# Four row tiles of activations in one tile, combined sets made 1280 columns at a time, and one accumulator copy moved to ScalarE

## The chip, the cores and the metric

The kernel runs on one core of one Trainium2 chip. The metric is the device time of one execution in microseconds; the figure for a kernel is the median of several runs. TensorE (PE) multiplies, VectorE (DVE) and ScalarE (ACT) do elementwise work, GpSimd (POOL) a little of it, and SyncE (SP) issues most DMAs. Each engine takes its instructions in the order in which they were written and waits on semaphores; here that order is written out by hand.

## The reference

One step of a hybrid diffusion backbone with one layer: 128 context tokens and 512 latent tokens, 640 in all, of 1024 channels, in float32.

```python
def trunk_layer(x, cond, ...):
    mod = jax.nn.silu(cond) @ w_mod + b_mod            # 9 vectors of 1024
    sh1, sc1, g1, shm, scm, gm, sh2, sc2, g2 = jnp.split(mod, N_MOD, axis=-1)
    h = modulate(rmsnorm(x, norm_g[0]), sh1, sc1)
    x = x + 0.5 * g1[:, None, :] * swiglu(h, ffn1_w1, ffn1_w2)     # 1024 -> 2 x 2816 -> 1024
    h = modulate(rmsnorm(x, norm_g[1]), shm, scm)
    y, C, n, m = mixer(h, ...)                         # w_in: 1024 -> 9232, mLSTM, conv, gates
    x = x + gm[:, None, :] * y
    h = modulate(rmsnorm(x, norm_g[2]), sh2, sc2)
    x = x + 0.5 * g2[:, None, :] * swiglu(h, ffn2_w1, ffn2_w2)
    return x, C, n, m
```

Context tokens use one conditioning vector and latent tokens another. A last RMSNorm ends it; the states of the mLSTM's context scan are outputs too.

## The kernel before

**Layout.** Activations lie transposed: 1024 channels are 8 row tiles (k = 0 to 7) of 128 partitions, 640 tokens are columns, cut into two halves (h = 0, 1) of 320 (`HT`). A matmul has 128 x 128 weights and 320 moving columns. Each float32 operand is split into a rounded high part and a remainder (`split`: a cast on ScalarE, L75, then a subtraction on VectorE, L79), and `three` makes one product out of three matmuls (L245 to L247).

**The pair element.** Most products with 1024 input channels come two column blocks at a time (`pair_el`, `pair_steps`), by a scheme of seven block products instead of eight. The activations are a 2 x 2 block matrix: blocks "11" and "21" (channels 0 to 511 and 512 to 1023 of half 0), "12" and "22" (the same of half 1). Besides these the scheme needs four combined sets, each of four row tiles: T1 = 12 - 11, T2 = 22 - T1, T3 = 22 - 12, T4 = 21 - T2. Weights are combined in the same way (L218) and split (L75, L79), four operands ahead of their use (`AHEAD`). A pair takes seven products of twelve matmuls, in the order A11, S1, S2, A12, S3, S4, A22, which use the activation sets 11, T1, T2, 21, T3, 22, T4. Between them accumulators are copied: after A11 its accumulator is copied to b (L273, ScalarE), on which S2 goes on; after S2, b is copied to c (L283, ScalarE), on which S3 and then A22 go on. After S3 the accumulator c is read, with S1's result added, into `c22`: by VectorE out of PSUM (L294), or with `spare_v` by a ScalarE copy (L291) and a VectorE addition (L292). A22 may write c only when that reading is done. `ev` then takes each result (L963 the silu on ScalarE, L965 the product on VectorE).

**The head of a stage.** Where a stage starts (first FFN, mixer, second FFN) the normalised activations are not ready yet, and the combined sets still have to be made. So the first blocks are made with plain products (`first_head` for the first FFN, `head_el` for the others): first half 0, then half 1, one unit of 24 matmuls for each block and half. While they run, `some`, called at two points of each unit, takes items off the list `work` that `right_chain` made: t1 (L905), the splits of T1, and so on, at a pace that spreads the list evenly over the points (12 in the first FFN, 10 in the others). In the first FFN the order is t1, T1, t3, T3, t2, T2, t4 and, after the head, T4. In the mixer and the second FFN it is t1, T1, t2, T2, t3, T3; t4 and T4 are in `N["later"]` and are issued (`fill`) between the products of the first pair. t2 is L908, t3 L911, t4 L914; t1, t2 and t4 are all made in place in one set `N["T"]`, t3 in place of half 1's channels 0 to 511. Items pushed on `lazy` (the splits of U, the gated products) go out at the next pair or step.

**Storage.** A row tile is one tile of 128 x 320, from rotating buffers: `utile` gives the normalised activations N[h, k] and N["T", k] (24 buffers, `Uh` and `Ul`, which the FFN's U tiles share), `hpair` the high and low tiles of a set (4 buffers each). The H tiles serve as scratch elsewhere: `YB` (mixer output), `h_wide` (accumulators), `FN` and `YT` (final norm).

Of the kernel before, what the change touches and what calls it, by code (L numbers as in the profile page):

```python
# [12 lines left out]
P = 128  # L13
# [31 lines left out]
def mixer_step(ctx: ExitStack, tc: tile.TileContext, x_prompt, x_sample, state_C, state_n, state_m,  # L45
# [28 lines left out]
    def split(raw, hi, lo, owe=False):  # L74
        A.copy(hi, raw)  # L75
        if owe:
            owed.append(lambda: V.tensor_sub(lo, raw, f32(hi)))
        else:
            V.tensor_sub(lo, raw, f32(hi))  # L79
# [693 lines left out]
    sq, SQ = {}, []  # L773
    PIECES = ((0, 128, 192), (320, 448, 512))
    OPS_H = ("11", "21", "22", "T1", "T2", "T3", "T4")
    cnt = {"u": 0}

    def utile():
        cnt["u"] += 1
        return PO["u"].tile([P, HT], F32, name=("Uh", "Ul")[cnt["u"] % 2], bufs=12)  # L780

    def hpool(o):
        return PO["hq"] if o in ("T1", "T2", "T3") else hp

    def hpair(o):
        return (hpool(o).tile([P, HT], F32R, name="H" + o + "h", bufs=4),
                hpool(o).tile([P, HT], F32R, name="H" + o + "l", bufs=4))

    def square(m, h):
        a, b = HALVES[h]  # L790
# [45 lines left out]
            PE.matmul(p[:, dst:dst + n], ones, dg[:, :n], start=True, stop=True)  # L836
        return p

    N = {}

    def scale_x(h, k, rb, engine=V):
        a, b = HALVES[h]
        t = utile()
        engine.tensor_mul(t, X[k][:, a:b], rb[:, :HT])  # L844
        N[h, k] = t

# [7 lines left out]
                V.tensor_scalar(t[:, a:b], t[:, a:b], sc_, bi_, op0=OP.mult, op1=OP.add)  # L854

    def put(o, kk, src):
        HB.setdefault(o, [None] * 4)[kk] = hl = hpair(o)
        split(src, *hl)

    def left_lists(n, sh):  # L860
        sc_ = lambda *ks: [lambda k=k: scale_x(0, k, N["rb", 0]) for k in ks]
# [16 lines left out]
    def right_chain(n, sh):  # L878

        def all_of(*fs):  # L880
            def f():
                for x in fs:
                    x()
            return f

        def right(k):
            if k < 4:
                HB.setdefault("12", [None] * 4)[k] = hl = hpair("T4")
                split(N[1, k], *hl)
            else:  # L890
                put("22", k - 4, N[1, k])

        def rows(k0, k1):

            for k in range(k0, k1):
                if k < KT:
                    scale_x(1, k, N["rb", 1])
                if 1 <= k <= KT:
                    modulate(1, k - 1, n, sh)
                if k >= 2:  # L900
                    right(k - 2)

        def t1(k):
            N["T", k] = utile()
            V.tensor_sub(N["T", k], N[1, k], N[0, k])  # L905

        def t2(k):
            V.tensor_sub(N["T", k], N[1, k + 4], N["T", k])  # L908

        def t3_(k):  # L910
            V.tensor_sub(N[1, k], N[1, k + 4], N[1, k])  # L911

        def t4(k):
            V.tensor_sub(N["T", k], N[0, k + 4], N["T", k])  # L914
        ks = range(4)
        work = [lambda k=k: t1(k) for k in ks] + [lambda k=k: put("T1", k, N["T", k]) for k in ks]
        work += [lambda k=k: t3_(k) for k in ks] + [lambda k=k: put("T3", k, N[1, k]) for k in ks]
        work += [lambda k=k: t2(k) for k in ks] + [lambda k=k: put("T2", k, N["T", k]) for k in ks]
        work += [lambda k=k: t4(k) for k in ks]
        last = [lambda k=k: put("T4", k, N["T", k]) for k in ks]  # L920
        if n in (1, 2):

            N["later"] = [all_of(*p) for p in zip(work[24:28:2], work[25:28:2])] + [all_of(*p) for p in zip(last[::2], last[1::2])]
            work, last = work[:8] + work[16:24] + work[8:16], []
        def fetch():

            if n == 2:
                A.activation(tp.tile([P, 3], F32, name="rstd", bufs=2)[:, 0:1], eps, AF.Silu)

        chain = [stat_fn(1), all_of(rows_fn(1), fetch, lambda: rows(0, 6)), lambda: rows(6, 9), lambda: rows(9, 10)]  # L930
        return chain + last, work
# [19 lines left out]
    def ffn(w1, w2, g, lists, head_of, n_head, e1=None):  # L951

        head, els, f0 = [], [], 0
        for size in GROUPS:
            U = {}
            grp = []
            for j in range(size):
                sa = {}

                def ev(mi, h, src, sa=sa, j=j, U=U):  # L960
                    if mi == 0:
                        sa[h] = t3()
                        A.activation(sa[h], src, AF.Silu)  # L963
                    else:
                        V.tensor_mul(sa[h], src, sa[h])  # L965

                        def put_u():
                            U[j, h] = hl = (PO["u"].tile([P, HT], F32R, name="Uh", bufs=12),
                                            PO["u"].tile([P, HT], F32R, name="Ul", bufs=12))
                            split(sa[h], *hl)  # L970
                        lazy.append(put_u)
                p = (w_load(w1, 0, KT, (f0 + j) * P, 2 * DFF), w_load(w1, 0, KT, DFF + (f0 + j) * P, 2 * DFF), ev)
                if f0 + j < n_head:
                    head.extend(blocks_of(p))
                else:
                    grp.append(pair_el(*p, e1 if f0 == 0 else None))
            acts = lambda k, h, U=U: U[k, h]
            ld = lambda m, f0=f0, size=size: w_load(w2, f0 * P, size, m * P, D)
            last = f0 + size == NFF
            w2s = [plain_el(ld(m), size, acts, lambda h, ps, m=m, last=last: add_x(m, h, ps, g, last))  # L980
                   for m in range(KT if not last else 2)]
            w2s[0] = dict(w2s[0], calm=False)
            if last:
                w2s.append(halves_el([ld(m) for m in range(2, KT)], size, acts,
                                     lambda m, h, ps: add_x(m + 2, h, ps, g, True), lists))
            els.append((grp, w2s))
            f0 += size
        return head_of(head), els
# [74 lines left out]
    def first_put(h, *ks):  # L1063
        for k in ks:
            if h == 0:
                put("11" if k < 4 else "21", k % 4, N[0, k])
            elif k < 4:
                HB.setdefault("12", [None] * 4)[k] = hl = hpair("T4")
                split(N[1, k], *hl)
            else:  # L1070
                put("22", k - 4, N[1, k])
# [786 lines left out]
    def sc_ev(m):  # L1858
        def ev(h, ps):
            g = GS[m][:, hsl(h)]  # L1860
            t = TL[m, h]
            V.tensor_mul(g, ps, g)
            V.scalar_tensor_tensor(t, t, 0.5, g, op0=OP.mult, op1=OP.add)
            if h == 0:
                return
            for i in range(2):
                YB[m, i] = hpair(YO[i][m // 4])
                split(TL[m, i], *YB[m, i])
            if m:
                x_in(m - 1)  # L1870
        return ev
# [5 lines left out]
    def m_wide():  # L1877
        return [xp.tile([P, T], F32, name="x", bufs=KT)[:, :512]]

    def h_wide():  # L1880
        return [hpool(o).tile([P, HT], F32, name="H" + o + "h", bufs=4)[:, :256] for o in ("T1", "T2")]

    def open_u2():
        m2.close()
# [36 lines left out]

    def fn_in():
        for q in range(4):
            t = hpool(OPS_H[q]).tile([P, HT], F32, name="H" + OPS_H[q] + "h", bufs=4)
            G.dma_start(t[:, :256], dap(final_norm, q * 256, [[0, P], [1, 256]]))
            FN.append(t)

    def y_part(m, h):
        def f():
            p = aux()  # L1930
            for i, a in enumerate(PIECES[h]):
                PE.transpose(p[:, i * P:(i + 1) * P], X[m][:, a:a + P], ident)
            q = m // 2
            for i in range(3):
                if h:
                    if m == 0:
                        YT[1, i] = ring.tile([P, 1024], F32, name="wr", bufs=RAWB)
                    V.tensor_mul(YT[1, i][:, m * P:(m + 1) * P], p[:, i * P:(i + 1) * P],
                                 FN[q][:, (m % 2) * P:(m % 2 + 1) * P])
                    continue  # L1940
                if m % 2 == 0:
                    YT[h, i, q] = hpool(OPS_H[q]).tile([P, HT], F32,
                                                       name="H" + OPS_H[q] + "h", bufs=4)
                V.tensor_mul(YT[h, i, q][:, (m % 2) * P:(m % 2 + 1) * P], p[:, i * P:(i + 1) * P],
                             FN[q][:, (m % 2) * P:(m % 2 + 1) * P])
        return f
# [41 lines left out]

    PO["y"] = y_queue
    head, els = ffn(ffn2_w1, ffn2_w2, G2, y_after, lambda bl: head_el(bl, *right_chain(2, SH2), mod_mid(G2, 0)), 2)  # L1990
    els[0][0][0]["fill"] = [step(f) for f in N["later"] + [lambda: None] * 6]
    prog += [head] + els[0][0] + [step(half_gate(G2))]
    for i in range(3):
        prog += els[i][1] + els[i + 1][0]
# [30 lines left out]
```

## Time and profile before

| | |
|---|---|
| median of 3 runs | 1662.68 us (1661.75 to 1663.08) |
| profiled execution | 1662.47 us, its span 1660.7 us |
| TensorE (PE) busy | 1641.4 us, 99%, 11189 matmuls |
| VectorE (DVE) busy | 1262.8 us, 76%, 2690 instructions |
| ScalarE (ACT) busy | 793.7 us, 48%, 1729 instructions |
| GpSimd (POOL) busy | 170.8 us, 10% |
| mean granted TensorE clock | 0.999 |

The span runs from the first to the last instruction. A row of the timeline begins with the start and the duration in us, then the engine, the line of the kernel, the operation, output tile <- input tiles, the shape and how many were merged into the row; in brackets stand the idle time of the engine before it and what ended that. In the groups by line the numbers behind the bar are busy us, mean ns of one, and idle time before. In a table of stages the columns are the span and the busy time of PE, its weight loads, DVE, ACT and POOL (with counts), the granted clock, the share of DMA and GB/s. Matmuls are pipelined and overlap, so their spacing is read from their starts.

### The profile page before, as it was taken

The page shows a single profiled execution, that of the slowest core. Times are in us where ns is not written, and L with a number is a line of the kernel's source. Part 1 is how long each engine was busy: PE and PEld are TensorE (multiplying, and loading weights), DVE is VectorE, ACT ScalarE, POOL GpSimd, SP SyncE. Part 2 cuts the span into 40 slices and gives each one's busy share as a digit, 9 for nine tenths or more (in the row PEclk, how much of TensorE's full clock was granted, in tenths as well). Part 3 has the DMA queues.
Part 4 walks back from the last instruction along what each step waited for, and adds up shares of the span by engine and source line. Part 5 has one row for each costly group of instructions (what it writes and reads, how often), then busy time and mean ns, then how long its engine had stood idle before and what let it go on. Part 6 is the DMA issues. An engine that isn't in the chain of part 4 may idle for free.

```text
span 1660.7 us, 29312 instructions
## 1 busy us (share of the span) xinstructions
PE 1641.4 (99%) x11189; PEld 1599.5 (96%) x11189; DVE 1262.8 (76%) x2690; ACT 793.7 (48%) x1729; POOL 170.8 (10%) x258
## 2 busy tenths in 40 slices
PE   8999999999999999999999999999999999999998
PEld 5999999999999999999999999999999999999997
DVE  6867877877778878778897898789598467476576
ACT  5642542533566656555561455532275245254253
POOL 2010000000031322111121221011100000000002
PEclk9999999999999999999999999999999999999999
DMA  9454343343352434342367323367232322233222
GB/s 321 114 163 122 105 124 111 102 130 100 108 182 82 113 88 108 73 113 67 96 205 238 110 78 90 105 194 209 90 102 78 101 77 78 75 91 88 77 77 64
DMA packets 273037, 193.08 MB, mean 116 GB/s; under 512 B 7924, under 2 KB 253051, under 8 KB 272897
## 3 DMA queue, kind: packets, MB, share of 16 engines
q1 hardware_dynamic: 263280, 158.36, 33.2%
q0 software_dynamic: 9584, 32.85, 6.8%
q8 instruction: 88, 1.44, 0.4%
q14 instruction: 53, 0.43, 0.1%
q10 hardware_dynamic: 32, 0.01, 0.0%
HBM read 175.87 MB, written 15.31 MB: 115 GB/s over the span
## 4 chain that ended last, share of the span: by engine, by line
PE 89%; DVE 4%; ACT 3%; DMA 2%; issue 1%; SPq 1%; POOL 0%; ACTq 0%; DVEq 0%; POOLq 0%
PE ps L245 27%; PE ps L246 27%; PE ps L247 27%; PE ax L1583 2%; PE ax L1614 2%; DMA wr<-in_ffn_w_dram 1%; PE ax L1586 1%; DVE wl L79 1%; PE ax L1560 1%; ACT Uh L852 1%; ACT wh L75 0%; SPq L552 0%; DVE x L937 0%; DMA wl<-in_x_sample_dram 0%; DVE Uh L844 0%
## 5 line engine op out<-in xcount | busy, mean ns | idle before, releaser
L79 DVE TENSOR_TENSOR wl<-wr,wh 128x512 fp32r<-128x512 f32 (+1 forms) x405 | 264.8, 668 | 80.5 <-ACT wh L75 77.4
L75 ACT CAST wh<-wr 128x512 fp32r<-128x512 f32 (+1 forms) x407 | 236.9, 593 | 157.6 <-PE ps L246 133.8
L79 DVE TENSOR_TENSOR wl<-ws,wh 128x512 fp32r<-128x512 f32 x292 | 206.0, 706 | 42.2 <-ACT wh L75 41.5
L75 ACT CAST wh<-ws 128x512 fp32r<-128x512 f32 x292 | 178.1, 619 | 103.5 <-DVE ws L218 64.6
L245 PE MATMUL ps<-Uh,wh 128*128 128x320 f32 x704 | 218.8, 311 | 0.0
L246 PE MATMUL ps<-Ul,wh 128*128 128x320 f32 x704 | 217.2, 308 | 0.0
L247 PE MATMUL ps<-Uh,wl 128*128 128x320 f32 x704 | 217.1, 308 | 0.0
L937 DVE SCALAR_TENSOR_TENSOR x<-ps,modT,x 128x128 f32<-128x128 f32 (+2 forms) x216 | 82.7, 433 | 113.9 <-PE ps L247 113.8
L245 PEld LDWEIGHTS ps<-Uh,wh 128*128 128x128 f32 x704 | 132.1, 188 | 1.2 <-issue 0.8
L246 PEld LDWEIGHTS ps<-Ul,wh 128*128 128x128 f32 x704 | 132.2, 188 | 0.2 <-DVE Ul L79 0.2
L247 PEld LDWEIGHTS ps<-Uh,wl 128*128 128x128 f32 x704 | 132.1, 188 | 0.0
L245 PE MATMUL ps<-HT4h,wh 128*128 128x320 f32 x376 | 118.6, 315 | 1.3 <-DVE t L294 1.3
L245 PE MATMUL ps<-H11h,wh 128*128 128x320 f32 x376 | 118.8, 316 | 0.5 <-ACT H11h L75 0.5
L245 PE MATMUL ps<-H21h,wh 128*128 128x320 f32 x376 | 117.7, 313 | 0.0
L246 PE MATMUL ps<-H11l,wh 128*128 128x320 f32 x376 | 116.5, 310 | 0.3
L246 PE MATMUL ps<-HT4l,wh 128*128 128x320 f32 x376 | 116.3, 309 | 0.1
L247 PE MATMUL ps<-H21h,wl 128*128 128x320 f32 x376 | 116.3, 309 | 0.0
L247 PE MATMUL ps<-HT4h,wl 128*128 128x320 f32 x376 | 116.2, 309 | 0.0
L247 PE MATMUL ps<-H11h,wl 128*128 128x320 f32 x376 | 116.2, 309 | 0.0
L246 PE MATMUL ps<-H21l,wh 128*128 128x320 f32 x376 | 116.1, 309 | 0.0
L245 PE MATMUL ps<-H22h,wh 128*128 128x320 f32 x344 | 107.6, 313 | 0.0
L246 PE MATMUL ps<-H22l,wh 128*128 128x320 f32 x344 | 106.6, 310 | 0.4
(440 smaller groups left out, 4489.1 us busy)
## 6 DMA issues: line engine op xcount, KB each, us to landing
wr<-in_ffn_w_dram SPq DMA_DIRECT2D x86, 512.0 KB, 3.9
wr<-in_w_in_dram SPq DMA_DIRECT2D x72, 512.0 KB, 3.9
wr<-in_w_mod_dram SPq DMA_DIRECT2D x51, 512.0 KB, 3.9
wr<-in_ffn_w_dram SPq DMA_DIRECT2D x48, 384.0 KB, 3.5
early<-in_w_mod_dram SPq DMA_DIRECT2D x13, 512.0 KB, 8.7
wr<-in_ffn_w_dram SPq DMA_DIRECT2D x20, 256.0 KB, 3.2
mg<-in_w_mod_dram POOLq DMA_DIRECT2D x8, 512.0 KB, 5.4
wr<-in_w_ml_out_dram SPq DMA_DIRECT2D x8, 512.0 KB, 4.4
```

The lines of the kernel that those rows point to most:

```text
L75: A.copy(hi, raw)
L79: V.tensor_sub(lo, raw, f32(hi))
L245: PE.matmul(ps, hi[:, ws], ah, start=start, stop=False, skip_group_check=True)
L246: PE.matmul(ps, hi[:, ws], al, start=False, stop=False, skip_group_check=True)
L247: PE.matmul(ps, lo[:, ws], ah, start=False, stop=stop, skip_group_check=True)
L852: A.activation(t[:, a:b], t[:, a:b], AF.Identity, scale=sc_, bias=bi_)
L937: V.scalar_tensor_tensor(X[m][:, o + a:o + b], ps[:, a:b], modT[:, g, m, cd:cd + 1], X[m][:, o + a:o + b], op0=OP.mult, op1=OP.add)
L1560: PE.matmul(p[:, :P], S["k", dt][:, sl], S["q", dt][:, sl], start=(dt == 0), stop=(dt == 1))
L1583: PE.matmul(p2[:, :DH + 1], S["q", dt][:, sl], S["C"][d][:, dt, :], start=(dt == 0), stop=(dt == 1))
L1586: PE.matmul(p1[:, :DH + 1], S["p", ch][:, d, :], PO["vt"][:, ch, :], start=True, stop=True)
L1614: PE.matmul(p[:, :DH + 1], kw[:, dt * P:(dt + 1) * P], PO["vt"][:, ch, :], start=True, stop=True)
```

## The change

It has three parts. First, four row tiles become one tile of 128 x 4 x 320: `uquad` in place of `utile` (6 buffers of four instead of 24) and `hquad` in place of four `hpair` tiles; a row tile is now a slice. The U tiles of one FFN block (high and low of both halves) are the four slices of one `uquad`. `h_wide`, `fn_in` and `y_part` use slices of quads. Second, t1 to t4 are each one instruction of 1280 columns, and so are the cast and the subtraction of the splits of T1 to T4 (`put_all`). The lists have 7 items (6 in the mixer and the second FFN) in place of 28 (24), paced over the same points. In the mixer's first pair T4 now comes one product earlier, as the list of fills is shorter; in the second FFN's first pair an empty step keeps T4 where it was. Third, the first pair of the second FFN gets `spare_v`.

```diff
-    def utile():
-        cnt["u"] += 1
-        return PO["u"].tile([P, HT], F32, name=("Uh", "Ul")[cnt["u"] % 2], bufs=12)
+    def uquad(dtype=F32):
+        return PO["u"].tile([P, 4, HT], dtype, name="U", bufs=6)
...
-    def hpair(o):
-        return (hpool(o).tile([P, HT], F32R, name="H" + o + "h", bufs=4),
-                hpool(o).tile([P, HT], F32R, name="H" + o + "l", bufs=4))
+    HQ = {}
+
+    def hquad(o, part="h", dtype=F32R):
+        return hpool(o).tile([P, 4, HT], dtype, name="H" + o + part)
+
+    def hpair(o, kk):
+        if kk == 0:
+            HQ[o] = hquad(o), hquad(o, "l")
+        return tuple(t[:, kk] for t in HQ[o])
...
     def scale_x(h, k, rb, engine=V):
         a, b = HALVES[h]
-        t = utile()
+        if k % 4 == 0:
+            NQ[h, k // 4] = uquad()
+        t = NQ[h, k // 4][:, k % 4]
...
+    def put_all(o, src):
+        q = hquad(o), hquad(o, "l")
+        HB[o] = [tuple(t[:, kk] for t in q) for kk in range(4)]
+        split(src, *q)
...
-        def t1(k):
-            N["T", k] = utile()
-            V.tensor_sub(N["T", k], N[1, k], N[0, k])
...
+        def t1():
+            NQ["T"] = uquad()
+            V.tensor_sub(NQ["T"], NQ[1, 0], NQ[0, 0])
+
+        def t2():
+            V.tensor_sub(NQ["T"], NQ[1, 1], NQ["T"])
+
+        def t3_():
+            V.tensor_sub(NQ[1, 0], NQ[1, 1], NQ[1, 0])
+
+        def t4():
+            V.tensor_sub(NQ["T"], NQ[0, 1], NQ["T"])
+        turn = lambda o: lambda: put_all(o, NQ[1, 0] if o == "T3" else NQ["T"])
+        work, last = [t1, turn("T1"), t3_, turn("T3"), t2, turn("T2"), t4], [turn("T4")]
         if n in (1, 2):
-            N["later"] = [all_of(*p) for p in zip(work[24:28:2], work[25:28:2])] + [all_of(*p) for p in zip(last[::2], last[1::2])]
-            work, last = work[:8] + work[16:24] + work[8:16], []
+            N["later"] = [t4, *last]
+            work, last = [t1, turn("T1"), t2, turn("T2"), t3_, turn("T3")], []
...
                         def put_u():
-                            U[j, h] = hl = (PO["u"].tile([P, HT], F32R, name="Uh", bufs=12),
-                                            PO["u"].tile([P, HT], F32R, name="Ul", bufs=12))
+                            if h == 0:
+                                U[j] = uquad(F32R)
+                            U[j, h] = hl = U[j][:, 2 * h], U[j][:, 2 * h + 1]
...
-                    grp.append(pair_el(*p, e1 if f0 == 0 else None))
+                    grp.append(pair_el(*p, e1 if f0 == 0 else None, spare_v=(n_head == 2 and f0 + j == n_head)))
...
     def h_wide():
-        return [hpool(o).tile([P, HT], F32, name="H" + o + "h", bufs=4)[:, :256] for o in ("T1", "T2")]
+        n = WIDE["n"]
+        WIDE["n"] += 1
+        if n % 2 == 0:
+            WIDE["q"] = hquad(("T1", "T2")[n // 2 % 2], dtype=F32)
+        return [WIDE["q"][:, 2 * (n % 2) + c, :256] for c in range(2)]
...
-            t = hpool(OPS_H[q]).tile([P, HT], F32, name="H" + OPS_H[q] + "h", bufs=4)
+            YT["q", q] = hquad(OPS_H[q], dtype=F32)
+            t = YT["q", q][:, 0]
...
-    els[0][0][0]["fill"] = [step(f) for f in N["later"] + [lambda: None] * 6]
+    els[0][0][0]["fill"] = [step(f) for f in N["later"][:1] + [lambda: None] + N["later"][1:] + [lambda: None] * 4]
```

More of the change, by code (lines that the diff above doesn't have):

```diff
@@ L775, in mixer_step @@
     OPS_H = ("11", "21", "22", "T1", "T2", "T3", "T4")
-    cnt = {"u": 0}
-    def utile():
-        cnt["u"] += 1
-        return PO["u"].tile([P, HT], F32, name=("Uh", "Ul")[cnt["u"] % 2], bufs=12)
+    def uquad(dtype=F32):
+        return PO["u"].tile([P, 4, HT], dtype, name="U", bufs=6)
     def hpool(o):
         return PO["hq"] if o in ("T1", "T2", "T3") else hp
-    def hpair(o):
-        return (hpool(o).tile([P, HT], F32R, name="H" + o + "h", bufs=4),
-                hpool(o).tile([P, HT], F32R, name="H" + o + "l", bufs=4))
+    HQ = {}
[5 more added lines that the diff above has]
+        return tuple(t[:, kk] for t in HQ[o])
     def square(m, h):
@@ L837, in spread @@
         return p
-    N = {}
+    N, NQ = {}, {}
     def scale_x(h, k, rb, engine=V):
         a, b = HALVES[h]
-        t = utile()
+        if k % 4 == 0:
+            NQ[h, k // 4] = uquad()
+        t = NQ[h, k // 4][:, k % 4]
         engine.tensor_mul(t, X[k][:, a:b], rb[:, :HT])
@@ L856, in put @@
     def put(o, kk, src):
-        HB.setdefault(o, [None] * 4)[kk] = hl = hpair(o)
+        HB.setdefault(o, [None] * 4)[kk] = hl = hpair(o, kk)
         split(src, *hl)
+    def put_all(o, src):
+        q = hquad(o), hquad(o, "l")
+        HB[o] = [tuple(t[:, kk] for t in q) for kk in range(4)]
+        split(src, *q)
     def left_lists(n, sh):
@@ L887, in right @@
             if k < 4:
-                HB.setdefault("12", [None] * 4)[k] = hl = hpair("T4")
+                HB.setdefault("12", [None] * 4)[k] = hl = hpair("T4", k)
                 split(N[1, k], *hl)
@@ L901, in rows @@
                     right(k - 2)
-        def t1(k):
-            N["T", k] = utile()
-            V.tensor_sub(N["T", k], N[1, k], N[0, k])
[L907 to L920, printed above, removed]
+        def t1():
[9 more added lines that the diff above has]
+        work, last = [t1, turn("T1"), t3_, turn("T3"), t2, turn("T2"), t4], [turn("T4")]
         if n in (1, 2):
-            N["later"] = [all_of(*p) for p in zip(work[24:28:2], work[25:28:2])] + [all_of(*p) for p in zip(last[::2], last[1::2])]
-            work, last = work[:8] + work[16:24] + work[8:16], []
+            N["later"] = [t4, *last]
+            work, last = [t1, turn("T1"), t2, turn("T2"), t3_, turn("T3")], []
         def fetch():
@@ L1067, in first_put @@
             elif k < 4:
-                HB.setdefault("12", [None] * 4)[k] = hl = hpair("T4")
+                HB.setdefault("12", [None] * 4)[k] = hl = hpair("T4", k)
                 split(N[1, k], *hl)
@@ L1866, in ev @@
             for i in range(2):
-                YB[m, i] = hpair(YO[i][m // 4])
+                YB[m, i] = hpair(YO[i][m // 4], m % 4)
                 split(TL[m, i], *YB[m, i])
@@ L1878, in m_wide @@
         return [xp.tile([P, T], F32, name="x", bufs=KT)[:, :512]]
+    WIDE = {"n": 0}
     def h_wide():
-        return [hpool(o).tile([P, HT], F32, name="H" + o + "h", bufs=4)[:, :256] for o in ("T1", "T2")]
+        n = WIDE["n"]
[3 more added lines that the diff above has]
+        return [WIDE["q"][:, 2 * (n % 2) + c, :256] for c in range(2)]
     def open_u2():
@@ L1941, in f @@
                 if m % 2 == 0:
-                    YT[h, i, q] = hpool(OPS_H[q]).tile([P, HT], F32,
-                                                       name="H" + OPS_H[q] + "h", bufs=4)
+                    YT[h, i, q] = YT["q", q][:, 1 + i]
                 V.tensor_mul(YT[h, i, q][:, (m % 2) * P:(m % 2 + 1) * P], p[:, i * P:(i + 1) * P],
```

## The prediction

> **What bounds the kernel now.** I read the page's busy times first, then the waits of TensorE, then the stretches around the three places where combined sets are made.
>
> ```profile
> span 1660.7 us, 29312 instructions
> ...
> PE 1641.4 (99%) x11189; PEld 1599.5 (96%) x11189; DVE 1262.8 (76%) x2690; ACT 793.7 (48%) x1729; POOL 170.8 (10%) x258
> ```
>
> TensorE is busy for all but 19.3 us of 1660.7, so shorter work on VectorE or ScalarE buys time only where TensorE waits for it. The profiled execution took 1662.47 us, 1.8 beyond its span and 0.2 under the median of the three runs (1662.68). The waits of TensorE on those two engines that involve products of the pair elements are two:
>
> ```profile
> PE ps L245 <- DVE t L294: 1.3, 1, 1.3
> ...
> PE ps L245 <- ACT ps L273: 0.4, 1, 0.4
> ```
>
> and the stages in which they lie, with the tail behind them (columns: span, PE, PEld, DVE, ACT, POOL busy, clock):
>
> ```profile
> 55.00:92.00 37.00, 36.62 (x246) 33.93 (x245) 31.89 (x67) 19.59 (x46) 1.58 (x3) 1.00 0.32 94
> ...
> 1210.00:1256.00 46.00, 44.68 (x317) 43.38 (x314) 41.40 (x95) 32.82 (x76) 0.00 (x0) 1.00 0.40 115
> ...
> 1653.00:1661.00 8.00, 0.27 (x3) 0.19 (x2) 1.96 (x6) 1.89 (x4) 0.00 (x0) 0.75 0.48 164
> ```
>
> In the first two rows TensorE is idle 0.38 and 1.32 us. Recovering both wins 1.7 us, 0.1% of the time; this is the ceiling of any gain. VectorE is at 86% and 90% there, so a loss has no such ceiling.
>
> **Part 1: 24 sets, four instructions become one.** In each of the three head stages four differences (t1 to t4) and four splits (a ScalarE cast, a VectorE subtraction) run on four row tiles of 320 columns. VectorE loses 24 x 3 = 72 instructions, ScalarE 12 x 3 = 36. What one of 1280 columns costs is worked out from shorter ones:
>
> ```profile
> 1252.30 0.68 DVE L79 TENSOR_TENSOR wl<-ws,wh 128x512 fp32r<-128x512 f32 x1
> 1252.90 0.48 DVE L294 TENSOR_TENSOR t<-ps,t 128x320 f32<-128x320 f32 x1
> 1253.31 0.48 DVE L79 TENSOR_TENSOR Ul<-t,Uh 128x320 fp32r<-128x320 f32 x1
> ```
>
> ```profile
> L75 ACT CAST wh<-ws 128x512 fp32r<-128x512 f32 x292 | 178.1, 619 | 103.5 <-DVE ws L218 64.6
> ```
>
> ```profile
> L75 ACT CAST Uh<-t 128x320 fp32r<-128x320 f32 x88 | 38.8, 452 | 8.1 <-DVE t L965 8.1
> ```
>
> VectorE steps 0.60 us behind 512 columns and 0.41 behind 320: 1.0 ns a column. My estimate for 1280 is a step of 1.40 us (1.48 to the result) where four steps took 1.6. The cast goes from 452 to 619 ns over 192 columns: 1.26 us for 1280. So 24 sets save VectorE about 24 x 0.2 = 5 us. The price is order: each engine works in order, and a split in four pieces ran as a relay (the subtraction of piece one beside the cast of piece two). In one piece the difference, the cast and the subtraction follow each other whole: 1.48 + 1.26 + 1.4 us, and what is queued behind the cast on ScalarE waits for a difference of 1280 columns, not of 320.
>
> The trace shows the fixed share by the rows above: 0.41 - 320 x 1.0 ns, some 0.08 us. [...]
>
> **First place, 55 to 92 us (first FFN).** Here the order is t1, T1, t3, T3, t2, T2, t4, T4, and the second half lies on the path:
>
> ```profile
> 72.20 0.49 DVE L908 TENSOR_TENSOR Ul<-Ul 128x320 f32<-128x320 f32 x1
> ...
> 74.21 0.49 DVE L965 TENSOR_TENSOR t<-ps,t 128x320 f32<-128x320 f32 x1
> ...
> 76.61 0.49 DVE L965 TENSOR_TENSOR t<-ps,t 128x320 f32<-128x320 f32 x1
> ...
> 78.62 2.49 DVE L79 TENSOR_TENSOR Ul<-t,Uh 128x320 fp32r<-128x320 f32 x6
> ```
>
> ```profile
> 75.58 0.46 ACT L75 CAST HT4h<-Ul 128x320 fp32r<-128x320 f32 x1 [2.00 <-DVE Ul L914]
> ...
> 77.16 2.26 ACT L75 CAST Uh<-t 128x320 fp32r<-128x320 f32 x6
> 79.32 0.61 ACT L75 CAST wh<-ws 128x512 fp32r<-128x512 f32 x1
> 79.84 0.41 ACT L273 COPY ps<-ps 128x320 f32<-128x320 f32 x1
> ```
>
> ```profile
> 79.63 0.30 PE L247 MATMUL ps<-HT1h,wl 128*128 128x320 f32 x1
> 80.31 0.42 PE L245 MATMUL ps<-HT2h,wh 128*128 128x320 f32 x1 [0.38 <-ACT ps L273]
> ```
>
> S2 (tile HT2) waits for the copy L273 of accumulator b; a matmul step is 0.147 us (1641.4 over 11189), so S2 is 0.53 late. On ScalarE the copy stands behind the T4 casts, six casts of U and one of a weight. Now, with 12 points for 7 items, t2 falls due at point 9, T2 at 11, t4 at 12, T4 after the loop. t2 takes the place of its second half: 72.20 to 73.60 (result 73.7). The T2 cast runs 73.7 to 75.0, since nothing else holds ScalarE (2.00 us of idle in the row); VectorE does L965 meanwhile and subtracts to 76.4; t4 to 77.8 (result 77.9). L965 lies beside the T4 cast, 77.9 to 79.2. Six casts in steps of 0.36 (from 2.26 for six) end at 81.35, the weight's 0.52 later, and the copy starts at 81.87 instead of 79.84: **+2.0 us**, straight onto S2. VectorE's U tiles and the sums behind them come 2.0 later too, but so does every product that uses them, so nothing more is late. Bounds: -0.53 (the stall goes) to +3.0 (five handovers between the engines, counted above at 0.1 us or less, at 0.3 each).
>
> **Second place, 494 to 528 us (mixer).** The order is t1, T1, t2, T2, t3, T3; t4 and T4 follow in the first pair.
>
> ```profile
> 515.38 1.28 ACT L1755 ACT_TABLE_LOAD   x1
> ```
>
> ```profile
> 517.42 0.69 DVE L79 TENSOR_TENSOR wl<-ws,wh 128x512 fp32r<-128x512 f32 x1 [0.94 <-ACT wh L75]
> ```
>
> T3 ends some 1.4 us later (the whole cast and what it no longer overlaps, as worked out for the third place), but VectorE idled 0.94 us here, behind a table load that does not depend on T3. T4 now comes one product earlier, two products ahead of need. Cost **0**, bounds -0.2 (its own 0.2 a set, if any is on the path) to +0.5 (the idle 0.94 does not cover all of 1.4).
>
> **Third place, 1210 to 1256 us (second FFN), with the ScalarE copy.**
>
> ```profile
> 1230.21 0.46 ACT L75 CAST HT1h<-Ul 128x320 fp32r<-128x320 f32 x1
> ...
> 1243.16 0.42 ACT L273 COPY ps<-ps 128x320 f32<-128x320 f32 x1
> ...
> 1250.97 0.62 ACT L75 CAST wh<-ws 128x512 fp32r<-128x512 f32 x1 [1.55 <-DVE ws L218]
> ```
>
> ```profile
> 1232.32 0.49 DVE L908 TENSOR_TENSOR Ul<-Ul 128x320 f32<-128x320 f32 x1
> ...
> 1243.77 0.48 DVE L965 TENSOR_TENSOR t<-ps,t 128x320 f32<-128x320 f32 x1
> ...
> 1250.20 0.68 DVE L218 TENSOR_TENSOR ws<-wr 128x512 f32<-128x512 f32 x1
> ```
>
> ```profile
> 1244.64 0.31 PE L245 MATMUL ps<-HT2h,wh 128*128 128x320 f32 x1
> ...
> 1251.97 0.31 PE L247 MATMUL ps<-H22h,wl 128*128 128x320 f32 x1
> 1253.53 0.39 PE L245 MATMUL ps<-HT4h,wh 128*128 128x320 f32 x1 [1.25 <-DVE t L294]
> ```
>
> A22 (HT4) starts 1.42 us late because VectorE, 90% busy in this stage, reads accumulator c only at 1252.90. With `spare_v` ScalarE copies c, and VectorE adds from SBUF when it comes to it. What is late next: T1's cast cannot start before 1230.21 as now, so T1 ends at 1230.21 + 1.26 + 1.4 = 1232.9 instead of 1232.3. Five instructions (L965, two sums, two weights, 0.4 + 4 x 0.6) bring t2 to 1235.7, t2 ends 1237.1; three more of 0.6 hide T2's cast; T2 ends 1240.3, one L965 1240.7, t3 1242.1. T3's cast then leaves VectorE idle to 1243.4, and T3 ends 1244.9 instead of 1243.77: VectorE is 1.1 us later. Copy b now ends at 1243.4 + 0.52 + 0.42 = 1244.35, still ahead of S2 at 1244.64. The four merged instructions t4 and T4 win 0.4 back, T4's cast being hidden. The sum L218 of 1250.20 comes at about 1251.0, the cast of 1250.97 behind it at 1251.7, and behind that the new copy of c ends near 1252.7: A22 starts at 1252.8, **-0.7 us**. Bounds: -1.42 (the copy is never late) to +1.1 (VectorE's delay reaches TensorE and the copy does not help). VectorE's add costs the same 0.48 either way.
>
> **Part 2: four tiles in one.** U, the H tiles, the wide accumulators and the output tiles become slices: no instruction and no DMA more or fewer, on the SP and POOL queues neither. A slice is tied up only by its own readers and writers, if slices are tracked one by one; the trace shows that they are, two engines working on one `wr` tile at once:
>
> ```profile
> 1653.82 1.48 DVE L1969 TENSOR_SCALAR wr<-wr,rstd 128x640 f32<-128x640 f32 x3
> 1653.82 1.63 ACT L1970 ACTIVATE wr<-wr,rstd 128x384 f32<-128x384 f32 x3 [0.24 <-DVE rstd L822]
> ```
>
> Its storage is freed as a whole, though. U of the last group is read half 0 first; its storage goes to the right half's N tiles, written only when the next head is four k steps (36 matmuls, 5.3 us) in, which is the cover. If it were gone, a refill would wait at most those 5.3 us. I take 0.
>
> **Sum:** 1662.47 + 2.0 + 0 - 0.7 = **1663.8 us**, 1.1 above the median.
>
> **The rivals.** (a) Saving alone: the relay does not matter, and both stalls go, -0.53 - 1.42: 1660.5. For it: VectorE at 90% and 5 us less work; against: the casts above wait for VectorE, not the reverse. It is still within 0.2%. (b) Slower: long casts hold accumulator copies in all three heads. The place is the copy L273 before S2. In the third head its margin is only 0.3 us; it decides when the T3 cast ends after 1243.7. Then each head pays the first one's 2.0, and the A22 gain is used up: 1662.47 + 6.0 = 1668.5. Against it: in the second head the table load orders the copy, not T3. (c) Whole tiles are tracked: TensorE would wait for the fourth split of a set where it now follows the first; the other three are 3 x 0.41 = 1.2 us behind. Once in each head, with the 2.0 of the first place, this gives 1662.47 + 3.7 + 2.0 = 1668.2. The row of `wr` speaks against. (d) The ScalarE copy does nothing, A22 waiting as long as now: 1664.5. (e) A clock drop. In the last 8 us TensorE idles 7.7 and its granted clock is 0.75, a loss of 2.0 us of clock. If the S2 stall, grown to 2.5 us, does the same, the time is 1665.8; against: in the two stages above the clock stays 1.00 over stalls of 0.5 and 1.4. [...]
>
> **How the numbers follow.** A measurement tells about 0.2%, 3.3 us, from no change. Chances: forecast 0.63, (a) 0.14, (b) 0.09, (c) 0.04, (d) 0.07, (e) 0.03. Forecast, (a), (d) and (e) end within 3.3 us; (b), (c) are slower: slower 0.12 with a little off the ends, same 0.85, faster 0.03. The bounds add up to -2.15 and +4.6, 1660.3 to 1667.1; I cut the top, where all must go wrong together: 1660.4 to 1666.6.
>
> **What would show it.** VectorE has 2618 instructions, ScalarE 1694. The wait of S2 on L273 in the first head grows to about 2.5 us, that on L294 vanishes, and A22 of the second FFN waits some 0.7 on a copy at L291. L905 to L914 show 128x1280 at 1.5 us and L75 at 1.26. I am wrong if the S2 wait stays near 0.5, or if a new wait on a split or an accumulator copy over 1 us stands in another head.

## The result and the profile after

The changed kernel takes 1664.68 us (median of 20 runs, 1663.8 to 1665.47), the kernel before 1662.24 us (20 runs, 1661.41 to 1664.08): a ratio of 1.0014, 95% interval [1.0008, 1.002]. The difference of 2.4 us is 0.15%, inside the 0.2% that I called no change, but on the slow side: the interval lies above 1, so a small loss is real. The forecast was 1663.8.

The head of the page after, then the waits of TensorE that involve pair elements (us in total, times, longest):

```profile
span 1663.0 us, 29194 instructions
...
PE 1642.0 (99%) x11189; PEld 1599.9 (96%) x11189; DVE 1259.0 (76%) x2618; ACT 791.1 (48%) x1694; POOL 172.0 (10%) x258
```

```profile
PE ps L245 <- ACT ps L273: 2.9, 2, 2.5
...
PE ps L245 <- ACT t L291: 0.5, 1, 0.5
```

VectorE has 72 instructions and 3.8 us of work less, ScalarE 35 instructions and 2.6 us less. TensorE waits longer all the same: the wait on VectorE's reading at L294 (1.3) is gone, a shorter one on the copy at L291 (0.5) stands in its place, and the wait on copy b (L273) has grown from 0.4 to 2.9, in two places where there was one. The stages (span, PE, PEld, DVE, ACT, POOL busy, clock):

```profile
55.00:92.00 37.00, 34.50 (x235) 33.22 (x235) 29.83 (x42) 17.65 (x34) 1.44 (x2) 1.00 0.32 93
494.00:528.00 34.00, 33.77 (x252) 30.71 (x252) 27.16 (x43) 23.50 (x43) 0.54 (x1) 1.00 0.39 103
1210.00:1256.00 46.00, 45.47 (x328) 43.38 (x327) 39.95 (x71) 32.26 (x66) 1.22 (x1) 1.00 0.39 115
```

In the first FFN TensorE is idle 2.50 us instead of 0.38, in the mixer 0.23 as before, in the second FFN's stage 0.53 instead of 1.32. The first FFN, ScalarE, VectorE and TensorE of the changed kernel:

```profile
74.00 1.26 ACT L75 CAST HT2h<-U 128x1280 fp32r<-128x1280 f32 x1 [2.85 <-DVE U L919]
78.40 1.26 ACT L75 CAST HT4h<-U 128x1280 fp32r<-128x1280 f32 x1 [3.14 <-DVE U L925]
79.57 2.25 ACT L75 CAST U<-t 128x320 fp32r<-128x320 f32 x6
81.72 0.61 ACT L75 CAST wh<-ws 128x512 fp32r<-128x512 f32 x1
82.24 0.41 ACT L273 COPY ps<-ps 128x320 f32<-128x320 f32 x1
```

```profile
75.29 1.49 DVE L79 TENSOR_TENSOR HT2l<-U,HT2h 128x1280 fp32r<-128x1280 f32 x1 [0.93 <-ACT HT2h L75]
76.82 1.49 DVE L925 TENSOR_TENSOR U<-U 128x1280 f32<-128x1280 f32 x1
78.23 0.48 DVE L972 TENSOR_TENSOR t<-ps,t 128x320 f32<-128x320 f32 x1
79.69 1.49 DVE L79 TENSOR_TENSOR HT4l<-U,HT4h 128x1280 fp32r<-128x1280 f32 x1 [0.98 <-ACT HT4h L75]
```

```profile
79.91 0.30 PE L247 MATMUL ps<-HT1h,wl 128*128 128x320 f32 x1
82.71 0.42 PE L245 MATMUL ps<-HT2h,wh 128*128 128x320 f32 x1 [2.50 <-ACT ps L273]
```

The two engines take turns: ScalarE idles 3.14 us for t4 (L925), then VectorE idles 0.98 for T4's cast. Behind that cast stand the six U casts, a weight's cast and copy b. S2 starts 2.80 us behind the last matmul of S1, 2.66 beyond a step of 0.147 (2.655 by the trace's unrounded times); before it was 0.53 beyond.

The second FFN, after: VectorE, ScalarE, TensorE.

```profile
1233.98 1.49 DVE L79 TENSOR_TENSOR HT1l<-U,HT1h 128x1280 fp32r<-128x1280 f32 x1 [1.60 <-ACT HT1h L75]
...
1246.02 1.49 DVE L79 TENSOR_TENSOR HT3l<-U,HT3h 128x1280 fp32r<-128x1280 f32 x1 [1.33 <-ACT HT3h L75]
```

```profile
1246.42 0.42 ACT L273 COPY ps<-ps 128x320 f32<-128x320 f32 x1
...
1254.22 0.62 ACT L75 CAST wh<-ws 128x512 fp32r<-128x512 f32 x1 [1.48 <-DVE ws L218]
1254.75 0.42 ACT L291 COPY t<-ps 128x320 f32<-128x320 f32 x1
...
1260.14 0.62 ACT L75 CAST wh<-ws 128x512 fp32r<-128x512 f32 x1 [0.35 <-DVE ws L218]
1260.67 0.42 ACT L273 COPY ps<-ps 128x320 f32<-128x320 f32 x1
```

```profile
1255.22 0.41 PE L245 MATMUL ps<-HT4h,wh 128*128 128x320 f32 x1 [0.46 <-ACT t L291]
...
1261.14 0.42 PE L245 MATMUL ps<-HT2h,wh 128*128 128x320 f32 x1 [0.38 <-ACT ps L273]
```

A22 waits 0.63 us instead of 1.42. What the prediction did not have is the last row: in the second FFN's second pair S2 now waits 0.55 us on copy b, which stands behind a weight's cast that waits for VectorE's sum at L218. The first two rows show VectorE idle for 1.60 and 1.33 us ahead of T1's and T3's subtractions.

### The profile page after: what moved, and what is told of

It is laid out like the page before. It is cut to its first block, busy times and chain, and to the rows that moved or that the text cites. A ratio compares the mean times of both kernels' runs of the same rounds, so it can differ in the third digit from the quotient of the medians.

```text
span 1663.0 us, 29194 instructions
## 1 busy us (share of the span) xinstructions
PE 1642.0 (99%) x11189; PEld 1599.9 (96%) x11189; DVE 1259.0 (76%) x2618; ACT 791.1 (48%) x1694; POOL 172.0 (10%) x258
## 4 chain that ended last, share of the span: by engine, by line
PE 90%; DVE 3%; ACT 3%; DMA 2%; issue 1%; SPq 0%; POOL 0%; ACTq 0%; DVEq 0%; POOLq 0%
PE ps L245 28%; PE ps L246 27%; PE ps L247 27%; PE ax L1591 2%; PE ax L1622 2%; PE ax L1594 1%; ACT U L858 1%; DMA early<-in_w_mod_dram 1%; DVE wl L79 1%; PE ax L1568 1%; DVE U L850 1%; DMA wr<-in_ffn_w_dram 0%; ACT wh L75 0%; DMA x<-rd 0%; DMA wl<-in_x_sample_dram 0%
## 5 line engine op out<-in xcount | busy, mean ns | idle before, releaser
L245 PE MATMUL ps<-U,wh 128*128 128x320 f32 x704 | 218.8, 311 | 0.0
L246 PE MATMUL ps<-U,wh 128*128 128x320 f32 x704 | 217.2, 308 | 0.0
L247 PE MATMUL ps<-U,wl 128*128 128x320 f32 x704 | 217.1, 308 | 0.0
L245 PEld LDWEIGHTS ps<-U,wh 128*128 128x128 f32 x704 | 132.1, 188 | 1.2 <-issue 0.8
L246 PEld LDWEIGHTS ps<-U,wh 128*128 128x128 f32 x704 | 132.2, 188 | 0.2 <-DVE U L79 0.2
L247 PEld LDWEIGHTS ps<-U,wl 128*128 128x128 f32 x704 | 132.1, 188 | 0.0
```

The costliest lines, as they stand in the source:

```text
L245: PE.matmul(ps, hi[:, ws], ah, start=start, stop=False, skip_group_check=True)
L246: PE.matmul(ps, hi[:, ws], al, start=False, stop=False, skip_group_check=True)
L247: PE.matmul(ps, lo[:, ws], ah, start=False, stop=stop, skip_group_check=True)
```

## The experiments

Waits below are from the start of one matmul to the start of the next, less the 0.147 us of a step. Each ratio is to runs of the kernel before that were taken beside the kernel's own; their median was 1662.08 for the first four experiments, 1662.01 for the next four, 1662.11 and 1662.31 for the last two pairs.

Four of the experiments cut the merged instructions up again. In them `cut_d` says in which heads the differences run tile by tile, `cut_s` in which heads the splits do; `n` is the head: 0 the first FFN, 1 the mixer, 2 the second FFN.

**First FFN's sets tile by tile again, the rest as changed.**

```diff
-        work, last = [t1, turn("T1"), t3_, turn("T3"), t2, turn("T2"), t4], [turn("T4")]
+        cut_d, cut_s = n in (0,), n in (0,)
...
+                    V.tensor_sub(NQ[o][:, sl], NQ[a][:, sl], NQ[b][:, sl])
+                return f
+            return [one(k, k == 0) for k in range(4)] if cut_d else [one(slice(0, 4), True)]
...
+            if cut_s:
+                return [lambda k=k: put(o, k, NQ[key][:, k]) for k in range(4)]
+            return [lambda: put_all(o, NQ[key])]
...
+        work, last = d1 + sets("T1") + d3 + sets("T3") + d2 + sets("T2") + d4, sets("T4")
```

> Theory 1 (the relay): in the first FFN one cast of 1280 columns waits for a difference of 1280 columns and holds the copy of accumulator b behind it; the storage is innocent. With the sets of the first FFN made tile by tile again, all else as in the changed kernel, S2 of its first pair waits 0.5 us instead of 2.66, and the time falls by 2.1 to about 1662.6. Rival (the storage): slices of one tile, freed as a whole, hold ScalarE or VectorE up. Then the S2 wait stays above 2 us and the time near 1664.7.

Measured: 1661.62 us (1661.19 to 1662.07), ratio 0.9997 [0.9989, 1.0006]. S2 of the first FFN waits 0.48; A22 of the second FFN 0.62 on L291 and its second pair's S2 0.53, as with the change. So the merged sets of the first FFN are the loss. The time is 3.1 below the changed kernel's, more than the 2.2 of that wait; part of the rest is the clock, below.

**The change without the ScalarE copy.**

```diff
-                    grp.append(pair_el(*p, e1 if f0 == 0 else None, spare_v=(n_head == 2 and f0 + j == n_head)))
+                    grp.append(pair_el(*p, e1 if f0 == 0 else None))
```

> The changed kernel without the ScalarE copy. Theory 1: VectorE, about 1 us behind its old place in the second FFN, reads accumulator c near 1256.2 on the changed kernel's clock, so A22 starts about 1.1 us later (wait 1.7 instead of 0.6), while the wait in the next pair (0.55) shrinks, since TensorE gives VectorE that time: net +0.6 to +1.1, 1665.3 to 1665.8. Rival (the copy does nothing): 1664.7.

Measured: 1665.87 us (1664.69 to 1668.99), ratio 1.0026 [1.0017, 1.0034]. A22 waits 2.18 on L294, 0.76 more than before the change: this is what VectorE's delay costs. The wait in the second pair is gone. The copy is worth 1.55 at A22 and gives 0.55 back one pair later. The time is 1.2 above the changed kernel's, more than the 1.0 of these waits; four of the 11 runs show a mean clock of 0.996 and average 1667.55 us, and this kernel has two long waits, 2.66 and 2.18 us. In its profile the clock stays at 1.00 behind both; behind waits of 2.02 and 2.66 us it fell to 0.50 in other profiles (below).

**The copy alone, on the kernel before.**

```diff
-                    grp.append(pair_el(*p, e1 if f0 == 0 else None))
+                    grp.append(pair_el(*p, e1 if f0 == 0 else None, spare_v=(n_head == 2 and f0 + j == n_head)))
```

> The kernel before with the ScalarE copy alone. Theory 1: the copy comes behind the cast that ends at 1251.6, so A22 waits 0.1 us or nothing instead of 1.42; up to 0.6 of it comes back as a wait in the next pair, where VectorE is still behind: 1660.8 to 1661.5. Rival (the copy does nothing, or VectorE's lateness is all paid later): 1662.2.

Measured: 1661.25 us (1660.28 to 1662.13), ratio 0.9995 [0.9986, 1.0004]. A22's wait is gone entirely (1.4), and S2 of the second pair waits 0.47: that wait comes with the copy, since the next pair is reached sooner while VectorE and the casts behind it are no earlier.

**The storage alone** (tiles of four, instructions of 320 columns, no copy).

```diff
+        cut_d, cut_s = n in (0, 1, 2), n in (0, 1, 2)
...
-                    grp.append(pair_el(*p, e1 if f0 == 0 else None, spare_v=(n_head == 2 and f0 + j == n_head)))
+                    grp.append(pair_el(*p, e1 if f0 == 0 else None))
...
-    els[0][0][0]["fill"] = [step(f) for f in N["later"][:1] + [lambda: None] + N["later"][1:] + [lambda: None] * 4]
+    els[0][0][0]["fill"] = [step(f) for f in N["later"] + [lambda: None] * 6]
```

> Four row tiles in one tile everywhere, but every instruction of 320 columns as before and no ScalarE copy. Theory 1: nothing changes, 1662.2, S2 of the first FFN waits 0.5 and A22 of the second 1.4, as before. Rival (the storage): 1663 to 1664.5, with new waits on splits.

Measured: 1662.18 us (1661.71 to 1662.8), ratio 1.0 [0.9992, 1.0009], waits as before (A22 1.41, S2 0.48). Tiles of four cost nothing; the rival of whole-tile tracking falls.

**Which half of a set costs: splits tile by tile, differences whole.**

```diff
+        cut_d, cut_s = n in (), n in (0, 1, 2)
```

> The differences stay one instruction of 1280 columns; the splits (ScalarE cast, VectorE subtraction) run tile by tile again in all three heads. Theory (handovers in whole sets, then the order on ScalarE): worked out from the rows of the changed kernel's execution, t2 ends at 73.6 us, its four subtractions at about 75.9, t4 at 77.3, the four T4 casts at 78.85, the six U casts at 81.0, copy L273 starts at about 81.5 (82.24 with both merged, 79.84 before): wait of S2 in the first FFN about 1.9 us instead of 2.66. In the second FFN the idle of VectorE ahead of T1's and T3's subtractions (1.60 and 1.33 us) falls below 0.5 each, so A22's wait falls from 0.63 to 0.3 or less. Time about 1663.4 us against 1664.7 with both merged. Rival (only the merged splits cost anything): S2's wait back to 0.5, time 1661.5.

Measured: 1665.33 us (1663.44 to 1666.32), ratio 1.0017 [1.0008, 1.0026]. S2 waits 2.74, no less than with both merged: the expectation of 1.9 failed, and the rival's 0.5 too. ScalarE's row in the first FFN:

```profile
78.17 1.54 ACT L75 CAST HT4h<-U 128x320 fp32r<-128x320 f32 x4 [2.66 <-DVE U L921]
79.62 2.25 ACT L75 CAST U<-t 128x320 fp32r<-128x320 f32 x6
```

The four casts start only when the whole t4 is through, only 0.23 us earlier than the single cast did, and then take 1.45 us in steps where it took 1.17. The relay is cut by either half alone. In the second FFN A22's wait does vanish; one of 0.85 us at S1 of the first pair, put down to T3's cast, takes its place, and S2 of the second pair still waits 0.29.

**The other half: differences tile by tile, splits whole.**

```diff
+        cut_d, cut_s = n in (0, 1, 2), n in ()
```

> The other half: the differences run tile by tile in all three heads, the splits stay one instruction of 1280 columns. Theory: T2's cast starts only when the fourth difference is through (73.8 us), VectorE idles until 75.1, T4's cast runs 78.1 to 79.4, copy L273 starts at about 82.0: S2's wait about 2.5 us, hardly less than the 2.66 of both merged; second FFN as with both merged (VectorE idle 1.3 ahead of T1 and T3, A22 0.5 to 0.7). Time about 1664.5 us. Rival (the wide differences are the larger half): S2's wait below 1.5, time below 1663.5.

Measured: 1666.04 us (1664.87 to 1667.72), ratio 1.0025 [1.0015, 1.0035]. S2 waits 3.13, against 2.5 expected: four differences take 1.6 us where one takes 1.4, and nothing is won for them. In the second FFN A22 waits 0.95, and S2 0.42 in the first pair and 0.53 in the second. The time was 1.5 above the expectation; behind the wait the granted clock is 0.50 for some microseconds (below).

**T4's split behind copy b.** The first FFN's T4 is moved out of the head to the first pair, as a fill.

```diff
-        last = right_chain(0, SH1)[0][4:]
+        N["t4"] = right_chain(0, SH1)[0][4:]
...
-            for f in work + last:
+            for f in work:
                 f()
...
+    first_pairs[0]["fill"] = [step(lambda: N["t4"][0]())] + first_pairs[0]["fill"]
```

> Only the place of T4's split in the first FFN is moved: from the end of the head to the first pair, behind copy b on ScalarE. All sets stay merged. Theory (the copy is late because it stands behind T4's cast and what follows it): S2's wait in the first FFN falls from 2.66 us to 0.5 or less, the second FFN keeps its two waits (A22 0.6, S2 of the second pair 0.5), time 1662.5 us (1664.7 less 2.2). Rival (VectorE is simply later by the merged sets, whatever stands ahead of the copy): S2 still waits over 1.5 us and the time stays over 1664.

Measured: 1663.5 us (1662.97 to 1664.86), ratio 1.001 [1.0001, 1.0019]. S2's wait is 0.06: what stands ahead of the copy on ScalarE is the cause, as the theory has it. The time misses by 1.0, for two new waits on TensorE:

```profile
88.69 0.41 PE L245 MATMUL ps<-HT4h,wh 128*128 128x320 f32 x1 [0.24 <-DVE t L294]
...
92.76 1.05 PE L574 MATMUL ax<-mg,cm 128*32 128x512 f32 x4 [1.06 <-DMA mg<-in_w_mod_dram]
```

The extra fill pushes the modulation's product (L574) one product on, so that its second half meets a weight that has not landed; and VectorE, now busy with T4 inside the pair, reads accumulator c late.

**The next difference ahead of a split, in all three heads.** All sets stay merged; in the first FFN t4 is written over its other operand, `NQ[0, 1]`.

```diff
-            V.tensor_sub(NQ["T"], NQ[0, 1], NQ["T"])
...
+            o = NQ[0, 1] if n == 0 else NQ["T"]
+            V.tensor_sub(o, NQ[0, 1], NQ["T"])
...
+        work, last = [t1, t3_, turn("T1"), turn("T3"), t2, t4, turn("T2")], [turn("T4")]
...
-            work, last = [t1, turn("T1"), t2, turn("T2"), t3_, turn("T3")], []
+            work, last = [t1, t3_, turn("T1"), t2, turn("T2"), turn("T3")], []
```

> All sets stay merged, but the next difference is issued ahead of a split instead of behind it, so that VectorE works on it while ScalarE casts: t1, t3, T1, T3, t2, t4, T2 and T4 in the first FFN (t4 written over its other operand), t1, t3, T1, t2, T2, T3 in the other two heads. Theory (the loss is VectorE's idle time in the handovers): VectorE t2 72.2 to 73.6, t4 to 75.0, T2's subtraction to 76.4; ScalarE casts T2 73.65 to 74.9 and T4 75.1 to 76.35, the six U casts to 78.5, copy L273 at 79.0, ahead of its 79.84 before: S2's wait 0 to 0.1 us. In the second FFN VectorE wins back some 2.5 us of idle: A22's wait 0.2 or less, S2 of the second pair 0.3 or less. Time 1660.6 us (1662.2 less both stalls of before), faster than both kernels. Rival (a cast of 1280 columns blocks ScalarE's queue whatever the order): S2's wait stays over 1.5 us, time over 1663.5.

Measured: 1660.65 us (1660.24 to 1661.54), ratio 0.9991 [0.9982, 1.0001]; S2 of the first FFN waits 0.12, both waits of the second FFN are gone. In the mixer t3 comes so early here that the gate products of half 1 read tiles that t3 has already overwritten: this part of the computation is changed, and the next kernel leaves the mixer's order alone.

**The same in the two FFN heads only**, with the mixer's list as in the changed kernel (`if n == 2:` around the second line above).

> All sets merged and the copy of c on ScalarE, as in the changed kernel; the next difference is issued ahead of a split in the two FFN heads only (t1, t3, T1, T3, t2, t4, T2, T4 in the first; t1, t3, T1, t2, T2, T3 in the second), the mixer's order stays as it was, since its gate products still read the tiles that t3 overwrites. Theory (the loss is VectorE's idle time in the handovers of the two FFN heads; the mixer never cost anything): waits as with the order changed in all three heads, S2 of the first FFN 0.1 to 0.15 us, A22 of the second FFN 0.2 or less, its second pair's S2 0.3 or less, time 1660.7 us, at least 1.0 below the kernel before. Rival (the mixer's order brought part of the gain): time 1661.3 or more, with a wait in 494 to 528 us that the other did not have.

Measured: 1660.95 us (1660.32 to 1662.49), ratio 0.9993 [0.9984, 1.0002]. S2 of the first FFN waits 0.12, A22 and the second pair's S2 do not wait; the mixer's order has no part in it, as its stage has 33.77 us of TensorE busy with the one order and with the other. ScalarE and the stages of this kernel:

```profile
74.02 1.26 ACT L75 CAST HT2h<-U 128x1280 fp32r<-128x1280 f32 x1 [2.85 <-DVE U L919]
75.87 1.26 ACT L75 CAST HT4h<-U 128x1280 fp32r<-128x1280 f32 x1 [0.59 <-DVE U L926]
...
79.72 0.41 ACT L273 COPY ps<-ps 128x320 f32<-128x320 f32 x1
```

```profile
55.00:92.00 37.00, 37.00 (x249) 34.23 (x247) 30.64 (x43) 18.45 (x35) 1.69 (x3) 1.00 0.32 96
...
1210.00:1256.00 46.00, 45.93 (x327) 44.82 (x324) 40.43 (x72) 32.66 (x66) 0.00 (x0) 1.00 0.41 115
```

T4's cast now follows T2's 1.85 us behind instead of 4.40, and copy b starts at 79.72, not 82.24 (the theory's 79.0 left out that ScalarE still waits 0.59 for t4). TensorE is busy for the whole of the first stage. This kernel has merged sets and the copy, and its median lies 1.2 us below the kernel before; the interval of the ratio still holds 1.

**The new order in the second FFN alone** (the list under `if n == 2:` without the change to the first FFN's).

> The new order in the second FFN's head alone; first FFN and mixer as in the changed kernel. Theory (two separate losses that add): S2 of the first FFN waits 2.6 to 2.7 us as with the change, A22 of the second FFN and its second pair's S2 together at most 0.3 (1.17 with the change), time 1664.7 - 0.9 to 1.2 = 1663.5 to 1663.8, with single runs up to 1 us above where TensorE's clock drops behind the long wait. Rival (the waits in the second FFN are made by the ScalarE copy and the weights, not by the idle relays): they stay at 0.5 and more each, time 1664.5 or more.

Measured: 1663.46 us (1662.8 to 1664.92), ratio 1.0008 [0.9999, 1.0017]; both waits of the second FFN are gone, S2 of the first FFN waits 2.66. So with the handovers filled these waits do not arise, and the two heads add.

**The clock.** In this profile the same wait of 2.66 us was followed by a granted clock of 0.68, where the changed kernel's had 1.00. Two more runs ask when that happens: the first FFN's fourth set alone tile by tile, for a shorter wait, and the changed kernel again.

```diff
-        work, last = [t1, turn("T1"), t3_, turn("T3"), t2, turn("T2"), t4], [turn("T4")]
+        work, last = [t1, turn("T1"), t3_, turn("T3"), t2, turn("T2"), all_of(*t4k)], [all_of(*T4k)]
```

> As the changed kernel, but the first FFN's fourth set alone (t4 and T4) runs tile by tile; T1 to T3 stay merged. Theory of the order on ScalarE: T4's casts run from 77.3 to 78.9 us instead of 78.40 to 79.57, the U casts follow, copy L273 starts at about 81.5: S2's wait about 1.95 us instead of 2.66, the second FFN's waits as with the change. Theory of the clock: a wait near 2.66 us is at the edge at which TensorE's granted clock falls behind it (it stayed at 1.00 in two profiled executions and fell in another with the same wait); below 2.0 us it stays at 1.00 in every run, so the single runs lie within some 1 us of each other, and the median is 1664.7 - 0.7, less some 0.4 for the runs with a drop: 1663.6 us. Rival for the clock (the spread comes from elsewhere): runs spread over 1.7 us as before, clock figures of 0.997 among them, median 1664.0.

> The changed kernel once more, unchanged, for its single runs and a second profile. Theory of the clock: the S2 wait of the first FFN is 2.66 us again; either the clock behind it is 1.00 and the run is near 1664.3, or it falls to between 0.5 and 0.75 for 2 to 5 us and the run is about 1 us longer; the single runs span 1663.8 to 1665.5, median 1664.7. Rival (the clock has no part): the mean clock of the single runs is the same in the faster and the slower half.

Measured: fourth set in pieces 1663.82 us (1663.18 to 1665.51 without one run of 4044.29, which the median has in it), ratio 1.0011 [1.0002, 1.002], S2's wait 2.02 us; the changed kernel again 1664.92 us (1663.93 to 1665.58), ratio 1.0015 [1.0006, 1.0024], wait 2.67 us. The stretches behind the wait, first of the changed kernel's first profile, then of its second, then of the kernel with T4 in pieces (the clock stands behind POOL's column):

```profile
82.00:85.00 3.00, 2.29 (x16) 1.92 (x20) 2.92 (x7) 1.42 (x4) 0.00 (x0) 1.00 0.00 0
85.00:88.00 3.00, 3.00 (x24) 2.34 (x17) 2.85 (x5) 1.84 (x5) 1.44 (x2) 1.00 0.83 203
```

```profile
83.00:84.00 1.00, 1.00 (x9) 1.00 (x8) 1.00 (x3) 0.00 (x0) 0.00 (x0) 0.92 0.00 0
84.00:85.00 1.00, 1.00 (x8) 0.67 (x11) 0.92 (x2) 0.99 (x3) 0.00 (x0) 0.50 0.00 0
85.00:86.00 1.00, 1.00 (x8) 0.08 (x8) 0.85 (x2) 1.00 (x3) 0.00 (x0) 0.50 0.62 172
86.00:87.00 1.00, 1.00 (x5) 0.25 (x2) 1.00 (x3) 0.34 (x1) 0.00 (x0) 0.50 1.08 320
87.00:88.00 1.00, 1.00 (x7) 1.00 (x8) 1.00 (x2) 0.00 (x0) 0.88 (x2) 0.87 0.59 163
```

```profile
82.00:85.00 3.00, 3.00 (x16) 2.35 (x19) 2.77 (x6) 1.75 (x5) 0.00 (x0) 0.61 0.15 38
85.00:88.00 3.00, 3.00 (x20) 1.74 (x13) 2.24 (x4) 0.58 (x2) 1.36 (x2) 0.82 0.84 233
```

The five one-microsecond rows fall short of a full clock by 0.08 + 0.50 + 0.50 + 0.50 + 0.13 = 1.71 us, which is 3.4 us at half speed; the last two rows give 3 x 0.39 + 3 x 0.18 = 1.71 again. TensorE's lag on the first profile grows from -0.22 to +1.32 us over this stretch; at the next product of L574, at 94 us, 0.58 comes back, so that 0.96 stays. So the clock is part of it, but my theory of an edge near 2.66 us falls: 2.02 was enough in one execution, and 2.66 was not in two others. In the 31 runs of the changed kernel the 11 with a mean clock of 0.999 average 1664.30 us, the 12 with 0.998 and the 8 with 0.997 average 1664.98 and 1665.09. The figure is coarse, since kernels without a long wait show 0.998 and 0.999 too, so the share of runs with a drop stays open; but a drop takes 1.71 of 1663 us, 0.001, from the mean, and the ends of the list, 0.8 us apart, suggest the price. By these figures it is part of the first experiment's extra gain and of the spread of the kernels with a long wait.

Why equal waits can differ is not shown. Behind 2.66 us the clock stays at 1.00 in the first profile of the changed kernel and in the profile of the kernel without the copy, which keeps it behind its 2.18 us too. Behind 2.66 us in the kernel with the new order in the second FFN alone, and behind 2.67 in the second profile of the changed kernel, it falls to 0.50.

## Why the prediction was right or wrong

**Right: the first FFN.** Predicted: S2 late by 2.0 us more, since its copy stands behind a relay in whole sets. Measured: 2.655 - 0.532 = 2.12. The copy started at 82.24, not 81.87: t2 began 0.28 later than the sum had it, and so did the matmuls ahead of S2 (79.91 for 79.63), which leaves 0.09 for the relay. The tile-by-tile kernel (wait 0.48) shows that merging is the cause, T4 behind the copy (0.06) that the order on ScalarE carries it.

**Right: the second FFN's A22.** Predicted -0.7, measured 0.63 - 1.42 = -0.79. The mechanism is that of the sum: the copy at L291 behind a cast that waits for L218. VectorE's delay there was 0.76 by the kernel without the copy, 1.1 - 0.4 in the sum.

**Right: mixer and storage at 0.** The mixer's stage has 33.77 us of TensorE before and after, and the storage alone gave a ratio of 1.0. Durations came out near the estimates: 1.49 us for 1280 columns on VectorE, 1.26 for the cast (the two rows that the cast was worked out from give 1.29). The saving on VectorE was taken too large: 3.8 us, not 24 x 0.2 = 5.

**Wrong: the term "-0.7 us" as the whole of the third place.** I followed the work to A22 and stopped there. The copy lets TensorE reach the next pair sooner, and copy b is not ready for it: S2 of the second pair waits 0.55, as it waits 0.47 with the copy alone and not at all without it. Net the place is worth -0.79 + 0.55 = -0.24, inside the bounds of -1.42 to +1.1 but a third of the term.

**Wrong: rival (e), a clock drop, at a chance of 0.03.** It happened in one of the two profiled executions of the changed kernel and, by the mean clocks, in a good part of its runs, at 0.8 us by those runs and 0.96 by the two profiles, not the 2.0 I took from the tail. My argument against it came from stalls of 0.5 and 1.4 us and could not reach 2.5. Waits of 2.02 to 3.13 us were followed by half clock in five profiled executions, two of 2.66 us were not.

**Sum.** From the median before: 1662.24 + 2.12 - 0.79 + 0.55 = 1664.1, against 1664.3 for the runs with the highest mean clock and a median of 1664.7. The forecast lacked the 0.55, and some 0.4 for the runs with a drop. It started from the profiled execution, 0.23 above that median, which hid a part of what it lacked; that was luck. The first profile has one more wait of 0.5 us, on ScalarE at L1815 (868 us), which the second profile of the same kernel lacks, so it is no part of the sum.

**The first rival, saving alone at 1660.5,** took it that the relay does not matter. The saving is real: 3.8 us of VectorE. It reached TensorE only in the order in which VectorE has a difference to do while ScalarE casts: 1660.95.

## What to carry to other kernels

Merging the steps of a relay between two in-order engines saved fixed cost on each here (3.8 us of VectorE, 2.6 of ScalarE) but made every handover as long as a whole step (ScalarE idle 3.14 us for t4, VectorE 0.98 for T4's cast); splitting one of the two engines' steps again did not bring the overlap back (S2 waited 2.74 and 3.13 us, 2.66 with both merged). Put independent work of the other set between a step and its answer instead (S2's wait 0.12 us, 1660.95 us), and only then merge. Follow a delay on a busy engine past the first wait that it reaches, to the next pair, and count with lost clock, in some executions, on top of a new stall of TensorE: 0.96 us between the two profiles of the changed kernel, whose stall was 2.66 and 2.67 us.

## What the runs showed of the hardware

TensorE's granted clock fell to 0.50 for 3.4 us behind waits of 2.02 to 3.13 us in five profiled executions, and stayed at 1.00 behind 2.66 us in two others, behind 2.18 us in the second FFN of the kernel without the copy, and behind 1.42 us in the kernel before. In the second profile of the changed kernel the drop begins 1.3 us after TensorE is back at work (work from 82.48, the first slow step at 83.77 us), so the wait and its price do not stand side by side in the trace. Between the two profiles of this kernel the drop costs 0.96 us of time, less than the 1.71 us of clock.
